# Two branch projections of a hybrid encoder, from 32-bit halves to scaled float16 halves

## The chip, the cores and the metric

One core of one Trainium2 chip runs the whole kernel. TensorE (PE) multiplies, with its weight loads shown as PEld; VectorE (DVE), ScalarE (ACT) and GpSimd (POOL) do the rest; SyncE (SP) issues nearly all DMAs, in the order of its own queue. The metric is the time of one execution on the device in microseconds, as the median of several runs.

## The reference, cut to what matters

One step of an encoder over 1024 prompt frames and 32 sample frames (1056 columns, `TT`), 1024 channels. Two branches are projected, mixed by sigmoid gates and projected once more:

```
def mixer_outputs(x, o_attn, conv, ga, gb, ma, mb, ln_g, ln_b, w_pa, w_pb, w_out):
    ya = (o_attn.reshape(B, T, ATTN_WIDTH) * jax.nn.silu(ga)) @ w_pa
    yb = (jax.nn.silu(layernorm(conv, ln_g, ln_b)) * jax.nn.silu(gb)) @ w_pb
    m = jax.nn.sigmoid(ma) * ya + jax.nn.sigmoid(mb) * yb
    return x + m @ w_out
```

All arrays are float32. `o_attn` comes from an attention with forget gates, `conv` from a causal depthwise convolution; `ga`, `gb`, `ma`, `mb` are columns of one input projection.

## The kernel before

Activations lie transposed: 128 channels by 1056 columns, eight such tiles `f` for 1024 channels. A product of 32-bit precision is made from halves: an operand is split into a high part `h` and a rest `l`, and `mms` issues for each of eight channel tiles `kt` the products wh·xh, wl·xh, wh·xl. An output tile is computed in three column pieces of 352 (`CH`), so 24 matmuls fill one PSUM bank piece and 72 one output tile.

Two kinds of halves are in use. The input projections (before about 1005 us) use float16 halves `xh`, `xl`: `Batch` squares and sums two weight tiles on ACT (`stage`), totals the sums over the partitions with a small PE matmul (`total`), takes a power of two from it on DVE (`power`), and makes scaled halves `wh` (`split`, on ACT, or on POOL where `sides["cast"]` says so) and `wl` (`rest`, three pieces on DVE); the result is scaled back by `inv` as the bank is read out. `begin` pops the next `Batch` from `plan` and spreads these steps over the beats of the product that runs (a beat, `beat`, is three matmuls). The last stages use 32-bit halves (F32R) that need no scaling: `split_w` copies a weight tile on ACT (L183) and subtracts on POOL in three pieces (L186).

The stages around the change:

- Until 980.5 us the attention runs, with 22 of 24 gate projections (`fills`) as filler between its matmuls. Its last matmuls are `po`; the gated results go to DRAM as `s_o` (L1336).
- From 980.5 us PE runs the last two fills, then `outproj("pa")`, then `outproj("pb")`, then the output projection (`Pair`, L1707). In this part only PE's order is written by hand; on the other engines and on SP a scheduler of the framework orders the instructions ahead of time.
- `a_half(f)` loads the attention's result from `s_o` into a buffer `a` (five such buffers, `bg`) and writes `ah` (ACT, L1515) and `al` (DVE, L1516).
- `ln_out(f)`, called in the course of `pa`, loads the convolution's `y` and the gate `g`, normalizes and multiplies in three DVE operations (L1524, L1525, L1528) and two Silu on ACT, and writes `c_h` on ACT (L1531) and `c_l` on POOL (L1532).
- `pa` multiplies its bank by (tanh(ma/2)+1) (`sma`, L1574) and stores it as `s_ya`; `pb` does the same with `mb` and adds `ya` (L1622, L1623), which gives twice the mixture. The factor 0.5 stands in the output stage (L1719, L1739).

Of the kernel before, what the change touches and what calls it, by code (L numbers as in the profile page):

```python
# [8 lines left out]
F32 = mybir.dt.float32  # L9
# [49 lines left out]
def build(tc, xT, xt, wv, wf, ckT, cv, clT, stT, vec, cst, yT, kT, vO, lfO, cpT, csT):  # L59
# [33 lines left out]
    class Batch:  # L93
# [34 lines left out]
        def total(self):  # L128
            pool, tag = totals[-1]
            held.add(id(self))  # L130
            self.ps = pool.tile([128, 512], F32, name="tot", tag=tag)
            if self.n == 2:
                nc.tensor.matmul(self.ps[:, :2], ones_b, self.topb, start=True, stop=True)
            else:
                for i in range(2):
                    nc.tensor.matmul(self.ps[:, 0:1], ones_b, self.topb[:, i:i + 1], start=(i == 0), stop=(i == 1))

        def power(self, ps=None, n=0):
            ps, n = (self.ps, self.n) if ps is None else (ps, n)
            held.discard(id(self))  # L140
            q, self.s, self.inv = [self.sc[:, 2 * i:2 * i + n] for i in range(3)]
            power(q, self.s, ps[:, :n], 77)
            nc.gpsimd.tensor_scalar(self.inv, q, back, 1.0, op0=ALU.mult, op1=ALU.mult)

# [139 lines left out]
    wx = pool("wx", 1, stack=pxp)  # L284
    xhome = [wx, wp, wp]
# [419 lines left out]
    makers += [lambda i=i: Batch(rest[i:i + 2]) for i in range(0, len(rest), 2)]  # L705
    rest = list(rest)
    plan.extend(m() for m in makers)
    firsts = {("ub", f) for f in range(1, 8)} | {("k", f) for f in range(8)} | set(rest[::2])
    totals.append((tr, "tr"))
    b1 = plan.pop(0)  # L710
# [785 lines left out]

    pjC = Banks3()
    bg = pool("bg", 5, stack=p3, side="right")
    rawp.extend(pool(f"rw{i}", 1, stack=p3, side="right") for i in range(2))
    psg2 = ExitStack()  # L1500
    sg2 = pool("sg2", 6, stack=psg2, side="right")
    whome[:] = [pool("w3", 1, stack=psg2, side="right"), wp, wp]

# [5 lines left out]
    nc.vector.tensor_mul(os_t, os_t, gs)  # L1509

    def a_half(f):
        a = big("a3")
        nc.sync.dma_start(a[:, :T], s_o[f, :, :T])
        nc.vector.tensor_copy(a[:, T:], os_t[:, f, :])
        nc.scalar.copy(ah[:, f, :], a)  # L1515
        nc.vector.tensor_sub(al[:, f, :], a, f32(ah[:, f, :]))  # L1516

    chl = []

    def ln_out(f):  # L1520
        y, g = big("y3"), big("g3")
        nc.sync.dma_start(y, s_y[f])
        nc.sync.dma_start(g, s_g["gb"][f])
        nc.vector.tensor_sub(y, y, mean)  # L1524
        nc.vector.tensor_mul(y, y, rstd)  # L1525
# [21 lines left out]
    def ln_step(f):  # L1547
        for g in LNO[f - 1]:
            ln_out(g)

    def outproj(g, rh, rl, mk, between=lambda f: None, order=range(8)):

        w = split_w(load_raw((g, order[0])))
        pss = [pjC.tile([128, CH], F32, name="pj", tag="pj") for _ in range(3)]
        for kt in range(KT):
            for c in range(3):
                mms(pss[c], w, rh, rl, csl(c), range(kt, kt + 1), kt == 0, kt == KT - 1)
        ev = mk(order[0])
# [8 lines left out]
    def mk_pa(f):  # L1567
# [4 lines left out]

        def ev(c, sl, ps):
            nc.vector.scalar_tensor_tensor(sma[c], sma[c], 1.0, ps, op0=ALU.add, op1=ALU.mult)  # L1574
# [39 lines left out]
    def mk_pb(f):  # L1614
        smb = mixed[f] = big("smb")
        nc.sync.dma_start(smb, s_g["mb"][f])
        nc.scalar.activation(smb, smb, AF.Tanh, scale=0.5)
        ya = big("ya")
        nc.sync.dma_start(ya, s_ya[f])

        def ev(c, sl, ps):
            nc.vector.scalar_tensor_tensor(smb[:, sl], smb[:, sl], 1.0, ps, op0=ALU.add, op1=ALU.mult)  # L1622
            nc.vector.tensor_add(smb[:, sl], smb[:, sl], ya[:, sl])  # L1623
            sm = slice(sl.start, min(sl.stop, HT if f < 4 else TT))
# [37 lines left out]
    class Pair:  # L1662
# [52 lines left out]
        def out(self, m, hf, x):  # L1715
            f = 2 * self.p + m

            def ev(sl, ps):
                nc.vector.scalar_tensor_tensor(x[:, sl], ps, 0.5, x[:, sl], op0=ALU.mult, op1=ALU.add)  # L1719
                nc.sync.dma_start(yT[f, :, hf * HT + sl.start:hf * HT + sl.stop], x[:, sl])  # L1720
# [6 lines left out]
        def first(self, w, x):  # L1727
            u = self.u
            yield from self.product(w, 0, quad(0, L), lambda sl, ps: nc.scalar.copy(u[:, sl], ps))
            later(3, lambda: nc.vector.scalar_tensor_tensor(x, u, 0.5, x, op0=ALU.mult, op1=ALU.add))  # L1730
            yield from self.product(w, 1, quad(4, L), self.out(0, 0, x))

        def second(self):
# [143 lines left out]
```

## Time and profile before

| | us |
|---|---|
| median of 3 runs | 1278.08 (1275.16 to 1278.91) |
| profiled execution, time on the device | 1275.56 |
| its span, first to last instruction | 1273.8 |
| PE busy | 1234.4 (97%) |
| DVE busy | 1009.4 (79%) |
| ACT busy | 745.7 (59%) |
| POOL busy | 628.5 (49%) |
| granted PE clock, mean | 0.993 |

A row of the groups has the line, engine, operation, output and input, the count, the busy time, the mean of one, and the idle time ahead. Matmuls overlap in the pipeline, so the time of one matmul (some 310 ns) is not its pitch: the pitch is read from starts that follow each other. The chain of waits names, from the end backwards, what the end waited for.

### The profile page before, as it was taken

The numbers are of one execution on the slowest core, as the hardware profiler recorded it, in microseconds if no ns is written. First come the engines' busy times: TensorE is split into PE (matmuls) and PEld (weight loads), VectorE is DVE, ScalarE is ACT, GpSimd is POOL, SyncE is SP. The second block draws the span as 40 slices with busy tenths as digits, with TensorE's granted clock in tenths as the row PEclk, the third lists the DMA queues.
The fourth block names the chain that finished last, engine by engine and source line by source line (L and its number), as shares of the span: only waits on it lengthen the run. The fifth ranks groups of instructions, "written<-read, shape, count | busy, mean of one in ns | idle before, by whom it ended". The sixth has DMA issues, their size and how long they took to land.

```text
span 1273.8 us, 24904 instructions
## 1 busy us (share of the span) xinstructions
PE 1234.4 (97%) x9276; PEld 924.3 (73%) x9276; DVE 1009.4 (79%) x1375; ACT 745.7 (59%) x1431; POOL 628.5 (49%) x579
## 2 busy tenths in 40 slices
PE   8999999999999999999999989989989999999998
PEld 5677786666666666666665655666656899999998
DVE  6799898888989989798998998876873694266764
ACT  6655655768677784456776666667764764233320
POOL 4058583728566561013554655534443285355662
PEclk9999999999999999999999999999999999999999
DMA  6345251423424247445989999989986987334462
GB/s 250 103 120 138 60 147 44 114 91 108 118 79 123 73 135 220 136 133 149 207 212 231 208 227 203 216 210 215 223 186 161 359 271 232 118 126 161 135 203 69
DMA packets 264410, 207.38 MB, mean 163 GB/s; under 512 B 186976, under 2 KB 228832, under 8 KB 264288
## 3 DMA queue, kind: packets, MB, share of 16 engines
q1 hardware_dynamic: 264144, 205.71, 59.7%
q8 instruction: 73, 1.20, 0.4%
q14 instruction: 49, 0.40, 0.1%
q10 hardware_dynamic: 144, 0.07, 0.0%
HBM read 110.84 MB, written 57.12 MB: 132 GB/s over the span
## 4 chain that ended last, share of the span: by engine, by line
PE 74%; DVE 9%; issue 5%; ACT 4%; DMA 3%; POOL 3%; SPq 0%; DVEq 0%; POOLq 0%; ACTq 0%
PE pj L194 53%; PE pjv L822 7%; PE pj L1707 6%; PE po L1319 2%; DVE wl L152 2%; DVE nm L1260 2%; DMA PT<-PH 2%; DVE PH L1290 2%; PE psS L1251 1%; POOL P L1287 1%; DVE y L386 1%; POOL PH L1288 1%; PE psS L1252 1%; ACT P L1266 1%; ACT PH L1281 1%
## 5 line engine op out<-in xcount | busy, mean ns | idle before, releaser
L194 PE MATMUL pj<-xl,wh 128*128 128x352 f16 (+2 forms) x1536 | 481.5, 313 | 1.3 <-DVE xl L608 1.3
L194 PE MATMUL pj<-xh,wh 128*128 128x352 f16 (+2 forms) x1536 | 481.9, 314 | 0.3 <-ACT xh L607 0.2
L194 PE MATMUL pj<-xh,wl 128*128 128x352 f16 (+2 forms) x1536 | 481.4, 313 | 0.1
L194 PEld LDWEIGHTS <-wh 128*128 128x128 f16 x3072 | 301.1, 98 | 163.1 <-issue 2.4
L386 DVE SCALAR_TENSOR_TENSOR y<-u,vec_t,y 128x1086 f32<-128x1086 f32 x240 | 358.2, 1493 | 4.0 <-ACT y L383 0.9
L194 PEld LDWEIGHTS <-wl 128*128 128x128 f16 x1536 | 150.5, 98 | 69.8 <-DVE wl L152 0.7
L1287 POOL TENSOR_SCALAR P<-P,nm 128x896 f32<-128x896 f32 (+3 forms) x64 | 66.7, 1042 | 188.0 <-ACT PH L1281 178.2
L152 DVE SCALAR_TENSOR_TENSOR wl<-raw,sc,wh 128x384 f16<-128x384 f32 x188 | 138.5, 758 | 23.5 <-ACT wh L149 22.2
L1266 ACT ACTIVATE P<-psS,nm 128x1024 f32<-128x1024 f32 (+7 forms) x128 | 94.5, 738 | 98.7 <-DVE nm L1260 36.7
L1260 DVE TENSOR_REDUCE nm<-psS 128x1 f32<-128x1024 f32 (+7 forms) x128 | 96.2, 751 | 44.8 <-PE psS L1253 28.3
L1281 ACT ACTIVATE PH<-P,nm 128x1024 f16<-128x1024 f32 (+7 forms) x128 | 98.5, 770 | 10.7 <-DMA PT<-PH 8.7
L186 POOL TENSOR_TENSOR wl<-raw,wh 128x384 fp32r<-128x384 f32 (+1 forms) x51 | 64.0, 1281 | 74.4 <-ACT wh L183 50.0
L1288 POOL TENSOR_TENSOR PH<-P,PH 128x896 f16<-128x896 f32 (+3 forms) x64 | 91.6, 1431 | 5.0
L953 POOL TENSOR_TENSOR sql<-sqf,sqh 128x352 fp32r<-128x352 f32 x48 | 53.2, 1108 | 68.0 <-ACT sqh L950 68.0
L1251 PE MATMUL psS<-KB,QB 128*128 128x512 f16 (+2 forms) x192 | 62.9, 328 | 18.6 <-ACT P L1266 18.4
L1290 DVE SCALAR_TENSOR_TENSOR PH<-P,nm,PH 128x896 f16<-128x896 f32 (+3 forms) x64 | 63.2, 988 | 15.0 <-ACT PH L1281 13.9
L822 PE MATMUL pjv<-vwh,xh 128*128 128x260 f16 x256 | 70.0, 274 | 0.0
L822 PE MATMUL pjv<-vwl,xh 128*128 128x260 f16 x256 | 70.0, 273 | 0.0
L822 PE MATMUL pjv<-vwh,xl 128*128 128x260 f16 x256 | 69.9, 273 | 0.0
L979 POOL TENSOR_TENSOR ql<-qn,qh 128x352 f16<-128x352 f32 (+1 forms) x48 | 62.7, 1321 | 9.4 <-ACT qh L978 9.2
L1319 PE MATMUL po<-PT,Vh 128*64 128x256 f16 (+1 forms) x640 | 58.2, 274 | 8.2 <-DMA PT<-PH 8.2
L120 ACT ACTIVATE junk<-raw 128x1024 bf16<-128x1024 f32 x62 | 65.1, 1049 | 0.1
(302 smaller groups left out, 2618.8 us busy)
## 6 DMA issues: line engine op xcount, KB each, us to landing
raw<-wf SPq DMA_DIRECT2D x92, 512.0 KB
kT<-kun SPq DMA_DIRECT2D x8, 528.0 KB
s_ga<-t SPq DMA_DIRECT2D x24, 176.0 KB
s_gb<-t SPq DMA_DIRECT2D x24, 176.0 KB
s_ma<-t SPq DMA_DIRECT2D x24, 176.0 KB
s_mb<-t SPq DMA_DIRECT2D x24, 176.0 KB
sma<-s_ma SPq DMA_DIRECT2D x24, 176.0 KB
y<-s_y SPq DMA_DIRECT2D x8, 528.0 KB
```

The lines of the kernel that those rows point to most:

```text
L152: nc.vector.scalar_tensor_tensor(wl[:, ks, :], raw[:, ks, :], self.s[:, i:i + 1], wh[:, ks, :], op0=ALU.mult, op1=ALU.subtract)
L194: nc.tensor.matmul(ps, a[:, kt, :], b(kt, sl), start=(first and n == 0), stop=(last and n == N - 1))
L386: t = nc.vector.scalar_tensor_tensor(y, u[:, i:i + CW], w, y, op0=ALU.mult, op1=ALU.add)
L822: nc.tensor.matmul(ps[:, :VC], a, b, start=(n == 0), stop=(n == 23))
L1260: nc.vector.tensor_reduce(self.nm[:, e:e + 1], self.ps[:, :self.w], axis=AX.X, op=ALU.max, negate=True)
L1266: nc.scalar.activation(self.P[:, :self.w], self.ps[:, :self.w], AF.Exp, bias=self.nm[:, e:e + 1], accum_out=self.nm[:, 2 + e:3 + e])
L1281: nc.scalar.mul(self.H[:, :n, 0, :], self.P3, self.f)
L1287: nc.gpsimd.tensor_scalar(self.P3, self.P3, f, 1.0, op0=ALU.mult, op1=ALU.mult)
L1288: nc.gpsimd.tensor_sub(self.H[:, :n, 1, :], self.P3, self.H[:, :n, 0, :])
L1290: nc.vector.scalar_tensor_tensor(self.H[:, :n, 1, :], self.P3, f, self.H[:, :n, 0, :], op0=ALU.mult, op1=ALU.subtract)
L1319: nc.tensor.matmul(po[64 * e:64 * e + 64, 128 * ii.start:256], v[:, j, 64 * e:64 * e + 64], pt[:, ii, e, j, x, :], start=(j == 0 and n == ...
L1707: nc.tensor.matmul(pss[c][:, :HC], a[:, k, :], x, start=(not more and kt == 0 and n == 0), stop=(kt == 3 and n == 2), skip_group_check=more)
```

## The change

Both branch projections get float16 halves of inputs and weights.

- The 16 weight tiles of `pa` and `pb` become eight more `Batch`es at the end of `plan`: squares on ACT, total on PE, `wh` on ACT, and `wl` now on DVE (L158 of the new kernel) where POOL made it before.
- The inputs get one scale for the whole operand (`Norm`): eight loads into eight `wide` buffers, eight squares on ACT with a sum, one PE matmul `ptot` over the sums (L1541), a reduction and two small steps on DVE, and only then eight high parts on ACT (L1548) and eight low parts on DVE (L1549). For `pa` this is emitted 18 beats before the end of the last fill; for `pb` in the second and third beat of output tile 6 of `pa`.
- `wide` is one set of eight buffers for both branches: a `y` of the convolution branch can be loaded only when the `a` of the same number has been split.
- `c_l` moves from POOL to DVE. The gate of `pb` is a Sigmoid instead of a Tanh, the scales back are multiplied in where `pb`'s banks are read (L1674, L1675), and the factor 0.5 leaves the output stage (three lines with a scalar become plain additions).

```diff
+        def square(self, f):
+            nc.scalar.activation(self.junk()[:, f, :].bitcast(BF16), self.x[f], AF.Square, accum_out=self.n8[:, f:f + 1])
+        def total(self):
+            ps = pjC.tile([128, CH], F32, name="ptot", tag="pj")
+            top, q, self.s = [self.sc[:, i:i + 1] for i in range(3)]
+            nc.tensor.matmul(ps[:, :8], ones_f, self.n8, start=True, stop=True)
+            nc.vector.tensor_reduce(top, ps[:, :8], axis=AX.X, op=ALU.add)
+            power(q, self.s, top, 77)
+            nc.gpsimd.tensor_scalar(self.back, q, 2.0 ** 100, 1.0, op0=ALU.mult, op1=ALU.mult)
+        def halves(self, h, l):
+            for f in range(8):
+                nc.scalar.mul(h[:, f, :], self.x[f], self.s)
+                nc.vector.scalar_tensor_tensor(l[:, f, :], self.x[f], self.s, h[:, f, :],
+                                               op0=ALU.mult, op1=ALU.subtract)
     def a_half(f):
-        a = big("a3")
+        a = norm_a.tile(f)
         nc.sync.dma_start(a[:, :T], s_o[f, :, :T])
         nc.vector.tensor_copy(a[:, T:], os_t[:, f, :])
-        nc.scalar.copy(ah[:, f, :], a)
-        nc.vector.tensor_sub(al[:, f, :], a, f32(ah[:, f, :]))
+        norm_a.square(f)
     def ln_out(f):
-        y, g = big("y3"), big("g3")
+        y, g = norm_c.tile(f), big("g3")
...
-        nc.scalar.copy(chl[0][:, f, :], y)
-        nc.gpsimd.tensor_sub(chl[1][:, f, :], y, f32(chl[0][:, f, :]))
+        norm_c.square(f)
     for f in range(8):
         a_half(f)
+    later(24 * len(fills) - 18, a_halves)
     while fills:
         last_gate()
...
+        if f == 6:
+            later(2, norm_c.total)
+            later(3, lambda: norm_c.halves(*chl))
     def outproj(g, rh, rl, mk, between=lambda f: None, order=range(8)):
-        w = split_w(load_raw((g, order[0])))
+        begin()
+        w = split.pop((g, order[0]))
...
-            nc.vector.scalar_tensor_tensor(smb[:, sl], smb[:, sl], 1.0, ps, op0=ALU.add, op1=ALU.mult)
-            nc.vector.tensor_add(smb[:, sl], smb[:, sl], ya[:, sl])
+            nc.vector.scalar_tensor_tensor(smb[:, sl], ps, inv, smb[:, sl], op0=ALU.mult, op1=ALU.mult)
+            nc.vector.scalar_tensor_tensor(smb[:, sl], ya[:, sl], sides["inv_a"][:, f:f + 1], smb[:, sl],
+                                           op0=ALU.mult, op1=ALU.add)
```

The scheduler makes new orders of SP, ACT and DVE from this. Two places matter.

SP at the end of the attention. Before, behind the last store `s_o<-ot` come two weight tiles, the sample gates `gs`, and the loads of `a` with other loads among them:

```order
L1336 DMA s_o<-ot 128x512
L175 DMA raw<-wf 128x1024 x2
L1508 DMA gs<-s_ga 128x8x32
L1513 DMA a_12871<-s_o 128x1024
L1044 DMA s_mb<-t 128x352
L1513 DMA a_12876<-s_o 128x1024
L1513 DMA a_12881<-s_o 128x1024
L1513 DMA a_12886<-s_o 128x1024
L1513 DMA a_12891<-s_o 128x1024
L175 DMA raw<-wf 128x1024
```

The same place on SP now, from the two weight tiles of the output projection (L181) on; `wide<-s_o` are the eight loads of `a`:

```order
L181 DMA raw<-wf 128x1024 x2
L1053 DMA s_mb<-t 128x352
L1345 DMA s_o<-ot 128x512
L1569 DMA g_13234<-s_gb 128x1056
L1569 DMA g_13355<-s_gb 128x1056
L1569 DMA g_13365<-s_gb 128x1056
L1569 DMA g_13475<-s_gb 128x1056
L1569 DMA g_13594<-s_gb 128x1056
L1053 DMA s_mb<-t 128x352
L1518 DMA gs<-s_ga 128x8x32
L1556 DMA wide<-s_o 128x1024 x6
L1053 DMA s_mb<-t 128x352
```

Five loads of `g`, which the convolution branch needs later, moved ahead of `gs` and of all loads of `a`; the last two loads of `a` follow the last row shown.

The low weight parts in the course of `pa`. Before, POOL made them, in turns with `c_l`:

```order
L1532 TENSOR_TENSOR c_l<-y_13183,c_h 128x1056
L186 TENSOR_TENSOR wl<-raw,wh 128x384 x2
L186 TENSOR_TENSOR wl<-raw,wh 128x256
L1532 TENSOR_TENSOR c_l<-y_13294,c_h 128x1056
L1532 TENSOR_TENSOR c_l<-y_13305,c_h 128x1056
L186 TENSOR_TENSOR wl<-raw,wh 128x384 x2
L186 TENSOR_TENSOR wl<-raw,wh 128x256
```

Now DVE makes them. Its rows for the second `Batch` of `pa` (output tiles 2 and 3), with the end of the convolution branch's work ahead of them (L1571 and L1574 are the products with `rstd` and `g`, L1626 reads `pa`'s banks, L175 is the scale of the weights):

```order
L1571 TENSOR_TENSOR wide<-wide,rstd 128x1056 x2
L1574 TENSOR_TENSOR wide<-wide,g_13475 128x1056
L1626 SCALAR_TENSOR_TENSOR sma<-sma,pj 128x352
L1574 TENSOR_TENSOR wide<-wide,g_13594 128x1056
L175 TENSOR_SCALAR sc<-sc 128x2
L1626 SCALAR_TENSOR_TENSOR sma<-sma,pj 128x352
L1574 TENSOR_TENSOR wide<-wide,g_13604 128x1056
L1574 TENSOR_TENSOR wide<-wide,g_13714 128x1056
L1574 TENSOR_TENSOR wide<-wide,g_13833 128x1056
L158 SCALAR_TENSOR_TENSOR wl<-raw,sc,wh 128x384 x2
L158 SCALAR_TENSOR_TENSOR wl<-raw,sc,wh 128x256
```

The low parts moved behind the whole convolution branch: between the scale of `a` and the first L158 row of this `Batch` DVE has the eight low parts of `a`, all 24 operations of L1570, L1571 and L1574, and the first six reads of `pa`'s banks. On PE, `ptot` stands behind 114 of the 168 matmuls of the fills that follow the last `po`; 54 more of the fills, 144 of output tiles 0 and 1, and one small total stand between it and the first matmul of output tile 2.

More of the change, by code (lines that the diff above doesn't have):

```diff
@@ L128, in total @@
         def total(self):
-            pool, tag = totals[-1]
+            pool, tag, width = totals[-1]
             held.add(id(self))
-            self.ps = pool.tile([128, 512], F32, name="tot", tag=tag)
+            self.ps = pool.tile([128, width], F32, name="tot", tag=tag)
             if self.n == 2:
@@ L142, in power @@
             power(q, self.s, ps[:, :n], 77)
-            nc.gpsimd.tensor_scalar(self.inv, q, back, 1.0, op0=ALU.mult, op1=ALU.mult)
+            g, f = self.keys[0][:2] if n == 2 else ("", 0)
+            if g == "pa":
+                self.inv = sides["inv_a"][:, f:f + 2]
+                later(8, lambda: nc.gpsimd.tensor_scalar(self.inv, q, sides["back_pa"], 0.5, op0=ALU.mult, op1=ALU.mult))
+            else:
+                nc.gpsimd.tensor_scalar(self.inv, q, sides["back_pb"] if g == "pb" else back, 1.0,
+                                        op0=ALU.mult, op1=ALU.mult)
         def high(self, i, wh, raw, ks):
@@ L277, in proj @@
             pass
+    pwx = ExitStack()
+    wx = pool("wx", 1, stack=pwx)
     pxp = ExitStack()
@@ L706, in build @@
     rest = list(rest)
+    last = [("pa", f) for f in range(8)] + [("pb", f) for f in PBO]
+    makers += [lambda i=i: Batch(last[i:i + 2]) for i in range(0, len(last), 2)]
     plan.extend(m() for m in makers)
-    firsts = {("ub", f) for f in range(1, 8)} | {("k", f) for f in range(8)} | set(rest[::2])
-    totals.append((tr, "tr"))
+    firsts = {("ub", f) for f in range(1, 8)} | {("k", f) for f in range(8)} | set(rest[::2]) | set(last[::2])
+    totals.append((tr, "tr", 512))
     b1 = plan.pop(0)
@@ L1497, in build @@
     pjC = Banks3()
+    totals.append((pjC, "pj", CH))
+    sides.pop("cast")
     bg = pool("bg", 5, stack=p3, side="right")
@@ L1500, in build @@
     psg2 = ExitStack()
+    pap = pool("pap", 1, stack=psg2, side="right")
+    ah = pap.tile([128, KT, TT], F16, name="ah")
+    al = pap.tile([128, KT, TT], F16, name="al")
     sg2 = pool("sg2", 6, stack=psg2, side="right")
-    whome[:] = [pool("w3", 1, stack=psg2, side="right"), wp, wp]
+    sides["inv_a"] = cp.tile([128, 8], F32, name="inv_a")
     def big(name):
@@ L1616, in mk_pb, with ev @@
         nc.sync.dma_start(smb, s_g["mb"][f])
-        nc.scalar.activation(smb, smb, AF.Tanh, scale=0.5)
+        nc.scalar.activation(smb, smb, AF.Sigmoid)
         ya = big("ya")
         nc.sync.dma_start(ya, s_ya[f])
-        def ev(c, sl, ps):
-            nc.vector.scalar_tensor_tensor(smb[:, sl], smb[:, sl], 1.0, ps, op0=ALU.add, op1=ALU.mult)
-            nc.vector.tensor_add(smb[:, sl], smb[:, sl], ya[:, sl])
+        def ev(c, sl, ps, inv):
+            nc.vector.scalar_tensor_tensor(smb[:, sl], ps, inv, smb[:, sl], op0=ALU.mult, op1=ALU.mult)
+            nc.vector.scalar_tensor_tensor(smb[:, sl], ya[:, sl], sides["inv_a"][:, f:f + 1], smb[:, sl],
+                                           op0=ALU.mult, op1=ALU.add)
             sm = slice(sl.start, min(sl.stop, HT if f < 4 else TT))
@@ L1729, in first @@
             yield from self.product(w, 0, quad(0, L), lambda sl, ps: nc.scalar.copy(u[:, sl], ps))
-            later(3, lambda: nc.vector.scalar_tensor_tensor(x, u, 0.5, x, op0=ALU.mult, op1=ALU.add))
+            later(3, lambda: nc.vector.tensor_add(x, x, u))
             yield from self.product(w, 1, quad(4, L), self.out(0, 0, x))
@@ L1738, in second @@
                 self.residual(m, hf, x)
-            half_of = lambda x, y: nc.vector.scalar_tensor_tensor(y, x, 0.5, y, op0=ALU.mult, op1=ALU.add)
+            plus = lambda x, y: nc.vector.tensor_add(y, y, x)
             sa, sb, z = [lambda i=i: self.w[i] for i in range(3)]
             yield from self.product(sa, 0, form(0), lambda sl, ps: nc.vector.tensor_add(u[:, sl], u[:, sl], ps))
-            later(4, lambda: half_of(u, x21))
-            later(5, lambda: half_of(u, x12))
+            later(4, lambda: plus(u, x21))
+            later(5, lambda: plus(u, x12))
             c = yield from self.product(sa, 1, form(1), lambda sl, ps: nc.vector.tensor_add(v[:, sl], u[:, sl], ps))
-            later(3, lambda: half_of(v, x22))
+            later(3, lambda: plus(v, x22))
             d = yield from self.product(sb, 0, quad(0, R), self.out(1, 1, x22))
```

37 lines of the change are left out of this document (25 added, 12 removed).

## Prediction

> **What bounds the kernel now.** I read the page's busy shares and its chain first, then the chain in order of time, then the stretches of the last 300 us.
>
> ```profile
> span 1273.8 us, 24904 instructions
> PE 1234.4 (97%) x9276; PEld 924.3 (73%) x9276; DVE 1009.4 (79%) x1375; ACT 745.7 (59%) x1431; POOL 628.5 (49%) x579
> PE 74%; DVE 9%; issue 5%; ACT 4%; DMA 3%; POOL 3%; SPq 0%; DVEq 0%; POOLq 0%; ACTq 0%
> 980.58 208.30 PE pj L194 x1320
> 1188.88 81.67 PE pj L1707 x672
> 1270.57 0.43 DVE r L1719
> ```
>
> From 980.58 us to the end the chain is PE alone: 1320 projection matmuls without a gap, then the 672 of the output projection. So a faster matmul here is worth its whole saving, and every wait of PE here is paid in full. The stretches (busy PE, PEld, DVE, ACT, POOL; clock, DMA share, GB/s) are the last fills, `pa` and `pb`:
>
> ```profile
> 980.60:1005.00 24.40, 24.40 (x165) 15.98 (x166) 10.48 (x16) 15.74 (x23) 5.45 (x6) 1.00 1.00 367
> 1005.20:1096.60 91.40, 91.40 (x577) 91.30 (x576) 58.51 (x49) 47.63 (x56) 54.03 (x29) 1.00 0.76 245
> 1096.70:1188.70 92.00, 92.00 (x580) 92.00 (x580) 49.50 (x69) 27.32 (x41) 46.49 (x43) 1.00 0.38 122
> ```
>
> PE is full in all three. DVE is at 58.51 of 91.40 us in `pa`, with POOL at 54.03. In the first stretch the DMA engines are full, at 367 GB/s: what is loaded there comes in the order in which SP asks for it.
>
> **The saving.** A matmul's pitch is read from starts and from evictions that follow each other. The first and the last of 45 float16 matmuls of 352 columns, and two evictions of `pb` that lie 48 of its 32-bit matmuls apart:
>
> ```profile
> 973.08 0.32 PE L194 MATMUL pj<-xh,wh 128*128 128x352 f16 x1
> 979.65 0.31 PE L194 MATMUL pj<-xl,wh 128*128 128x352 f16 x1
> 1135.50 0.52 DVE L1622 SCALAR_TENSOR_TENSOR smb<-smb,pj 128x352 f32<-128x352 f32 x1 [0.16 <-PE pj L194]
> 1143.13 0.52 DVE L1622 SCALAR_TENSOR_TENSOR smb<-smb,pj 128x352 f32<-128x352 f32 x1 [2.73 <-PE pj L194]
> ```
>
> Float16: 6.57 us over 44 steps, 149.3 ns. 32-bit: 7.63 us over 48, 159.0 ns. Two branches of 576 matmuls: 1152 x 9.7 ns = 11.2 us saved. This shape in float16 is in this trace, so the price is sure to some tenths of a us. The output projection stays 32-bit and saves nothing.
>
> **The first wait: the scale of `a`.** `ptot` stands behind 114 matmuls of the last fills: 980.5 + 114 x 0.1493 = 997.5 us. It needs the squares of all eight tiles of `a`, so the last load of `a` must have landed. Before, no PE instruction needed that so early:
>
> ```profile
> 981.13 0.32 SPq L1336 DMA_DIRECT2D s_o<-ot  x1
> 983.27 0.33 SPq L1513 DMA_DIRECT2D a<-s_o  x1
> 998.21 0.85 SPq L1513 DMA_DIRECT2D a<-s_o  x2
> 989.45 1.07 ACT L1515 CAST ah<-a 128x1056 fp32r<-128x1056 f32 x1 [0.88 <-DMA s_mb<-t]
> 1006.79 1.06 ACT L1515 CAST ah<-a 128x1056 fp32r<-128x1056 f32 x1
> a<-s_o SPq DMA_DIRECT2D x8, 512.0 KB
> raw<-wf SPq DMA_DIRECT2D x5, 512.0 KB
> g<-s_gb SPq DMA_DIRECT2D x3, 528.0 KB
> s_mb<-t SPq DMA_DIRECT2D x12, 176.0 KB
> s_o<-ot SPq DMA_DIRECT2D x2, 256.0 KB
> gs<-s_ga SPq DMA_DIRECT2D x1, 128.0 KB
> ```
>
> The first copy of `a` began at 989.45, the last at 1006.79. In the new order of SP there stand, up to and with the last load of `a`: two `raw` (1024 KB), three `s_mb` (528), `s_o` (256), five `g` (2640), `gs` (128) and eight `a` (4096): 8672 KB, 8.88 MB. At the 367 GB/s of the full stretch this takes 24.2 us, from 981.1 (when the last `s_o` can go, which ends the attention) to 1005.3; with one square (the 1.07 us of the same shape) the sum is there at 1006.4. The wait is 1006.4 - 997.5 = 8.9 us. The other bound: before, 2048 KB of `raw`, `gs`, the eight `a`, 1056 of `sma`, 528 of `s_mb` and `s_o` (8112 KB, 8.31 MB) took from 981.1 to 1006.8, which is 323 GB/s since loads from behind take a share; at that rate the sum comes at 1009.7, a wait of 12.2 us. I take 10, nearer the first, because the loads of `a` now follow each other closely; range 5.5 to 13. The Trainium skill (DMA: Bandwidth & Descriptors, Bandwidth) measured 425 GB/s for 16 MB. By that, an estimate, the wait would be 20.9 + 1.07 + 981.1 - 997.5 = 5.6 us and the whole 4.4 us less; the full stretch of this trace shows 367, and I keep that.
>
> **The second wait: the low weight parts of output tile 2.** From `ptot` to the first matmul of output tile 2 PE has 198 matmuls: 198 x 0.1493 = 29.6 us. DVE does its rows in order, and its first L158 row of that `Batch` stands behind the convolution branch. Prices:
>
> ```profile
> L1516 DVE TENSOR_TENSOR al<-a,ah x8: 1258/1259/1259, 990.6 to 1007.9; 128x1056 fp32r<-128x1056 f32 x8
> L1525 DVE TENSOR_TENSOR y<-y,rstd x8: 1244/1446/2069, 1011.2 to 1058.2; 128x1056 f32<-128x1056 f32 x8
> L1574 DVE SCALAR_TENSOR_TENSOR sma<-sma,pj x24: 506/511/524, 1016.5 to 1097.4; 128x352 f32<-128x352 f32 x24
> L152 DVE SCALAR_TENSOR_TENSOR wl<-raw,sc,wh x188: 464/612/2727, 10.9 to 976.1; 128x384 f16<-128x384 f32 x126, 128x256 f16<-128x256 f32 x62
> 998.05 0.88 ACT L1571 ACTIVATE sma<-sma 128x352 f32<-128x352 f32 x2
> 1029.77 1.25 DVE L1525 TENSOR_TENSOR y<-y,rstd 128x1056 f32<-128x1056 f32 x1
> 1030.93 0.51 DVE L1574 SCALAR_TENSOR_TENSOR sma<-sma,pj 128x352 f32<-128x352 f32 x1
> ```
>
> ACT has three Tanh of `sma` (0.49 each) and the first high part (1.07) ahead of DVE's first low part: 2.5 us. Then eight low parts of `a`: not in the trace in this form; at the 1.26 of L1516, 10.1 us. Then 24 operations at 1.25 us, the least of L1525, since POOL, with its 54.03 busy us beside that line's spread to 2.069, has almost nothing left here: 30.0. Six reads of banks at 0.51: 3.1. One low weight piece: 0.5. Sum 46.2, a wait of 16.6 us. Where operations follow each other freely the next starts some 0.08 us ahead of the printed end (1029.77 and 1030.93: 1.16 apart), which takes up to 2.5 us off: 14.1. With 1.446 for the 24 it would be 4.7 more: 21.3. I take 15.5: most rows wait for nothing, some for a row just ahead. This wait does not depend on the first, because both sides start at `ptot`.
>
> **The clock.** What a wait of over 3 us does to PE is in the trace:
>
> ```profile
> 936.70 0.31 PE L194 MATMUL pj<-xl,wh 128*128 128x352 f16 x1
> 940.54 0.58 PE L1251 MATMUL psS<-KB,QB 128*128 128x512 f16 x1 [3.53 <-ACT P L1266]
> 941.45 0.50 PE L194 MATMUL pj<-xh,wh 128*128 128x352 f16 x1
> 941.75 0.50 PE L194 MATMUL pj<-xh,wl 128*128 128x352 f16 x1
> 940.60:943.90 3.30, 3.30 (x20) 1.61 (x20) 1.75 (x3) 1.96 (x6) 0.00 (x0) 0.50 0.90 223
> 944.00:947.00 3.00, 3.00 (x22) 1.84 (x20) 1.99 (x4) 2.15 (x6) 1.36 (x2) 1.00 0.65 109
> ```
>
> After 3.53 us of idle time the granted clock is 0.50 until about 944 and 1.00 behind it; the same matmuls start 0.30 us apart instead of 0.149. 3.4 us at half speed are a loss of 1.7 us. After the first wait this loss lies beside DVE's work and only shortens the second wait; after the second it is paid. I add 1.7 (0 to 3.4). The Trainium skill (TensorE: Matmul & The Clock Gate, Part 1) has the gate look at free-running windows of about 3.4 us, so that a restart can fall inside one. By that, an estimate, up to two windows would run at half speed and the sum would be 1.7 us higher; the trace shows one.
>
> **What costs nothing, and its cover.** Squares and high parts of the weights on ACT (16 times two of about 1.05 us, less 16 copies it loses): ACT has 44 us free in `pa` and 65 in `pb`. Low weight parts later on, 2 x 1.9 us for each two output tiles of 21.5 us: DVE is free once the convolution branch is done. The scale of `c`: its squares end with the convolution branch, before output tile 3, and its eight high and low parts (8 x 1.26 = 10.1 us on DVE) have the 46 beats from the second of tile 6 to the end of `pa`, 46 x 0.448 = 20.6 us; if that cover went, PE would wait at the head of `pb` by what is over. Late reads of `pa`'s first banks: six of eight banks are held at the most, so PE finds one. Sigmoid for Tanh, a scalar form for an addition, additions for scaled ones in the output stage: the same shapes at 0.51 to 0.53 us, off the chain. Loads of `y` now wait until `a` is split; the first is asked for at the first low part's end and read four low parts (5 us) later.
>
> **Sum.** 10 + 15.5 + 1.7 - 11.2 = +16.0 us. Against the profiled execution, 1275.56, this gives 1291.6; the median of the runs shown is 1278.08, 2.5 higher. I say 1292.
>
> **The rivals.**
> Not slower: the second wait does not come, because DVE, with POOL quiet, does its 32 full-width operations faster than any row of before. It decides below (29.6 - 2.5 - 3.1 - 0.5) / 32 = 0.73 us each. Then 10 + 1.7 - 11.2 = +0.5: 1276, no change. Against it: the least of L1525 is 1.244 and that of L1516 1.258, with POOL idle beside some of them. 5 in 100.
> The first wait is small: the five `g` need nothing from the attention, and if their buffers come free early they are loaded while the DMA engines idle before 981. Without their 2.7 MB the sum is there 7.4 us earlier: 1284. Against it: SP asks in order, and they stand behind the last `s_o`. 15 in 100.
> The `y` come late: the first product of the convolution branch stands between the fifth and sixth low part of `a` on DVE; behind six `sma` and two `raw` (2.1 MB, 5.7 us at 367 GB/s) the first `y` may land 3 to 5 us after it is wanted, and everything behind it on DVE, with it the second wait, is longer by that: 1296. For it: the queue is full there. Against it: those eight are asked for during the first wait. 17 in 100.
> The matmuls don't gain: 32-bit ones carry their weight load, float16 ones have it as an instruction of its own. Then 1303. Against it are the 149.3 ns, with just such loads. 3 in 100.
>
> **How the numbers follow.** The forecast has 60 in 100. Its own ends are 5.5 + 14.1 - 11.2 = +8 and 13 + 21.3 + 3.4 - 11.2 = +26; the likely part and the two neighbouring rivals lie within 1284 and 1300, which I give as the range. 0.3% (some 4 us, about what a measurement of this kernel tells from no change) divides the rest: faster 3 in 100 (both waits far off at once), the same 5, slower 92.
>
> **What would show it.** Right: PE idle for about 10 us ahead of `ptot` near 997.5, its releaser ACT or a load of `a`; idle for about 15 us ahead of the first matmul of output tile 2, its releaser a low weight part on DVE, with DVE busy all the while; matmuls of both branches 149 ns apart; no wait at the head of `pb`. Wrong: DVE idle inside the second wait (the `y` are late), a `g` landed before 981 (the first wait shrinks), or a pitch near 159.

## Result, and the profile after

The changed kernel takes 1296.92 us (median of 4 runs, 1295.92 to 1299.53) against 1277.87 (4 runs) of the kernel before on the same chip: ratio 1.0156, 95% interval 1.0133 to 1.0178, 19.05 us slower. The forecast was 1292, the range 1284 to 1300.

The profiled execution took 1299.53 us, the slowest of the four. Part of that lies ahead of the change. These are the last matmuls of the attention, first in the kernel before, then after (start, duration, engine, line, operation, output and input):

```profile
980.35 0.22 PE L1319 MATMUL po<-PT,Vh 128*64 128x128 f16 x2
```

```profile
985.09 0.22 PE L1328 MATMUL po<-PT,Vh 128*64 128x128 f16 x2
```

Up to this row the two kernels do nearly the same work, and it came 4.74 us later in this one execution; in other runs of the changed kernel's variants it came at 979.0 to 983.9. So stages are compared from this row to the end of the span: 1273.8 - 980.35 = 293.4 us before, 1297.7 - 985.09 = 312.6 after. The difference, 19.2 us, agrees with that of the medians; this stretch is "the tail" below. PE's waits in the tail after the change (engine, line waited for, total, times, longest):

```profile
PE pj L200 <- ACT wh L155: 12.6, 1, 12.6
PE ptot L1541 <- ACT ah L1536: 11.7, 1, 11.7
PE pj L200 <- DVE wl L158: 0.2, 1, 0.2
```

Before there was none. The stretches of the tail after the change (columns as in the prediction):

```profile
985.50:1002.40 16.90, 16.90 (x115) 10.88 (x112) 0.74 (x2) 9.84 (x13) 0.00 (x0) 1.00 0.96 325
1002.40:1014.10 11.70, 0.05 (x2) 0.00 (x1) 4.03 (x17) 10.77 (x19) 0.00 (x0) 0.63 1.03 403
1014.70:1024.82 10.12, 10.12 (x55) 5.98 (x53) 8.71 (x10) 9.95 (x13) 0.46 (x2) 0.78 0.79 266
1044.50:1059.70 15.20, 2.46 (x15) 1.18 (x12) 13.38 (x18) 13.79 (x20) 2.38 (x1) 0.67 0.79 237
1059.70:1127.00 67.30, 67.24 (x442) 43.60 (x443) 28.57 (x54) 36.29 (x51) 1.56 (x7) 0.97 0.47 152
1127.00:1212.30 85.30, 85.30 (x577) 56.06 (x575) 56.47 (x98) 31.81 (x50) 22.93 (x28) 1.00 0.38 118
```

The second row is the first wait: PE idle, DMA full, ACT busy for 10.77 of 11.70 us. The fourth holds the second wait. Behind each the granted clock is under 1.00. The last row is `pb` without its first six matmuls. From the start of its first matmul to the start of its last, `pb` takes 85.9 us (1126.08 to 1211.97); before, it took 91.4 (1097.15 to 1188.56). The groups give its pitch: one of the three kinds of matmul, first and last start.

```profile
L200 PE MATMUL pj<-c_l,wh x192: 311/313/313, 1126.4 to 1212.0; 128*128 128x352 f16 x192
```

85.6 us over 573 steps are 149.4 ns. The saving is there in full; the waits cost more.

The first wait, row by row, on SP, ACT, DVE, ACT again and PE:

```profile
988.28 0.38 SPq L1345 DMA_DIRECT2D s_o<-ot  x1
994.19 1.28 ACT L1573 ACT_TABLE_LOAD   x1 [4.61 <-DMA g<-s_gb]
1000.70 1.08 ACT L1573 ACTIVATE g<-g 128x1056 f32<-128x1056 f32 x1 [0.32 <-DMA g<-s_gb]
1002.00 0.42 DVE L1519 TENSOR_TENSOR os_t<-os_t,gs 128x256 f32<-128x256 f32 x1 [16.16 <-DMA gs<-s_ga]
1003.34 1.08 ACT L1536 ACTIVATE ah<-wide 128x1056 bf16<-128x1056 f32 x1 [1.11 <-DVE sc L174]
1004.42 2.17 ACT L155 ACTIVATE wh<-raw,sc 128x1024 f16<-128x1024 f32 x2
1012.88 1.07 ACT L1536 ACTIVATE ah<-wide 128x1056 bf16<-128x1056 f32 x1
1014.10 0.60 PE L1541 MATMUL ptot<-n,ones_f 128*128 128x8 f32 x2 [11.65 <-ACT ah L1536]
```

The last `s_o` goes out at 988.28, 3.2 us after the attention's last matmul. On ACT a table load and the five Silu of the early `g` come first, from 994.19 to 1001.78. The sample gates `gs` land at 1002.0, the first square of `a` starts at 1003.34, and from there ACT runs without a gap: a square, two high weight parts, seven squares 1.06 us apart, none of which waits for a load. `ptot` comes when that row is through, 11.65 us after PE was ready.

The second wait: DVE's groups from 1016.6 to 1057.2 us, that whole stretch, and the rows around its end.

```profile
L1549 DVE SCALAR_TENSOR_TENSOR al<-wide,nsc,ah 128x1056 f16<-128x1056 f32 x8 | 10.1, 1311 | 1.3 <-ACT ah L1548 1.3
L1571 DVE TENSOR_TENSOR wide<-wide,rstd 128x1056 f32<-128x1056 f32 x8 | 9.9, 1250 | 0.0
L1570 DVE TENSOR_TENSOR wide<-wide,mean 128x1056 f32<-128x1056 f32 x8 | 9.8, 1251 | 0.0
L1574 DVE TENSOR_TENSOR wide<-wide,g 128x1056 f32<-128x1056 f32 x8 | 9.8, 1249 | 0.0
```

```profile
1016.60:1057.20 40.60, 29.89 (x193) 19.05 (x191) 40.60 (x40) 31.17 (x41) 3.32 (x2) 0.88 0.67 218
```

```profile
1053.69 3.59 DVE L1574 TENSOR_TENSOR wide<-wide,g 128x1056 f32<-128x1056 f32 x3
1057.92 2.17 ACT L155 ACTIVATE wh<-raw,sc 128x1024 f16<-128x1024 f32 x2
1059.09 3.00 DVE L158 SCALAR_TENSOR_TENSOR wl<-raw,sc,wh 128x384 f16<-128x384 f32 x6 [1.81 <-ACT wh L155]
1059.11 0.47 PE L200 MATMUL pj<-ah,wh 128*128 128x352 f16 x1 [12.62 <-ACT wh L155]
1059.76 0.47 PE L200 MATMUL pj<-ah,wl 128*128 128x352 f16 x1 [0.18 <-DVE wl L158]
```

DVE is busy for 40.60 of 40.60 us with the low parts of `a` and the convolution branch. Its row ends at 1057.3; ACT's high part begins at 1057.92, DVE's low part at 1059.09. PE is let go by the high part, so the page names ACT, but the two engines end within 2 us of each other. Which one holds the other, the page can't say.

### The profile page after: what moved, and what is told of

It reads as the page before. It is cut to its first block, busy times and chain, and to the rows that moved or that the text cites. A ratio compares the mean times of both kernels' runs of the same rounds, so it can differ in the third digit from the quotient of the medians.

```text
span 1297.7 us, 24983 instructions
## 1 busy us (share of the span) xinstructions
PE 1230.8 (95%) x9288; PEld 856.4 (66%) x9288; DVE 1021.6 (79%) x1453; ACT 781.3 (60%) x1495; POOL 558.0 (43%) x541
## 4 chain that ended last, share of the span: by engine, by line
PE 68%; DVE 10%; DMA 6%; issue 5%; ACT 5%; POOL 4%; SPq 1%; DVEq 0%; POOLq 0%; ACTq 0%
PE pj L200 48%; PE pjv L831 7%; PE pj L1761 6%; DMA PT<-PH 2%; PE po L1328 2%; POOL PH L1297 2%; DVE wl L158 2%; DVE nm L1269 1%; PE psS L1260 1%; DVE y L393 1%; PE psS L1261 1%; DVE PH L1299 1%; ACT PH L1290 1%; POOL P L1296 1%; ACT P L1275 1%
## 5 line engine op out<-in xcount | busy, mean ns | idle before, releaser
L200 PEld LDWEIGHTS <-wh 128*128 128x128 f16 x3840 | 377.5, 98 | 216.8 <-ACT wh L155 13.0
L200 PEld LDWEIGHTS <-wl 128*128 128x128 f16 x1920 | 188.5, 98 | 90.3 <-DVE wl L158 1.5
L158 DVE SCALAR_TENSOR_TENSOR wl<-raw,sc,wh 128x384 f16<-128x384 f32 (+1 forms) x236 | 167.7, 740 | 37.0 <-ACT wh L155 36.9
L1290 ACT ACTIVATE PH<-P,nm 128x1024 f16<-128x1024 f32 (+7 forms) x128 | 98.5, 770 | 12.1 <-DMA PT<-PH 10.2
L120 ACT ACTIVATE junk<-raw 128x1024 bf16<-128x1024 f32 x78 | 81.9, 1050 | 24.6 <-DMA raw<-wf 24.3
L962 POOL TENSOR_TENSOR sql<-sqf,sqh 128x352 fp32r<-128x352 f32 x48 | 56.6, 1182 | 64.8 <-ACT sqh L959 64.8
L200 PE MATMUL pj<-ah,wh 128*128 128x352 f16 x192 | 60.9, 317 | 12.6 <-ACT wh L155 12.6
L155 ACT ACTIVATE wh<-raw,sc 128x1024 f16<-128x1024 f32 (+1 forms) x58 | 64.2, 1123 | 14.3 <-DVE sc L175 14.3
L126 POOL CAST topb<-tops 128x2 bf16<-128x2 f32 x32 | 15.6, 488 | 131.3 <-ACT junk L120 131.1
```

Source lines behind the costliest of these rows:

```text
L120: nc.scalar.activation(junk[:, :raw.shape[1] * raw.shape[2]], raw.rearrange("p a b -> p (a b)"), AF.Square, accum_out=self.tops[:, i:i + 1])
L158: nc.vector.scalar_tensor_tensor(wl[:, ks, :], raw[:, ks, :], self.s[:, i:i + 1], wh[:, ks, :], op0=ALU.mult, op1=ALU.subtract)
L200: nc.tensor.matmul(ps, a[:, kt, :], b(kt, sl), start=(first and n == 0), stop=(last and n == N - 1))
L1290: nc.scalar.mul(self.H[:, :n, 0, :], self.P3, self.f)
```

## Experiments

The theory at this point: the change saves 11.2 us and pays for two rows that PE never waited for before, ACT's squares behind late loads (first wait) and DVE's convolution branch ahead of the weights' parts (second wait). Rivals: the late `gs` makes the first wait; ACT, not DVE, makes the second. The runs below were taken on several chips, so between rows the ratio and the tail compare better than the median.

| kernel | median us (range, runs) | ratio to before on the same chip (95%) | tail us |
|---|---|---|---|
| before | 1277.87 (1275.16 to 1278.91, 4) | | 293.4 |
| after | 1296.92 (1295.92 to 1299.53, 4) | 1.0156 (1.0133 to 1.0178) | 312.6 |
| `g` behind `a` | 1292.41 (1291.33 to 1294.27, 4) | 1.0119 (1.0100 to 1.0138) | 308.3 |
| weights first | 1284.00 (1282.17 to 1290.26, 5) | 1.0070 (1.0043 to 1.0096) | 299.4 |
| both | 1284.84 (1280.99 to 1285.28, 7) | 1.0045 (1.0030 to 1.0060) | 299.6 |
| `gs` early | 1296.49 (1293.80 to 1298.98, 4) | 1.0149 (1.0127 to 1.0171) | 313.0 |
| no squares of `c` | 1296.66 (1295.53 to 1298.88, 4) | 1.0145 (1.0128 to 1.0161) | 311.9 |
| DVE one less | 1290.30 (1289.27 to 1292.39, 4) | 1.0097 (1.0078 to 1.0116) | 306.2 |
| both, head of `pb` | 1276.58 (1273.10 to 1278.09, 12) | 0.9980 (0.9970 to 0.9990) | 291.6 |
| later total | 1273.85 (1271.22 to 1275.35, 6) | 0.9962 (0.9948 to 0.9977) | 289.6 |
| total 3 beats later | 1274.46 (1270.04 to 1278.06, 9) | 0.9973 (0.9955 to 0.9992) | 288.8 |
| total 5 beats later | 1275.20 (1272.26 to 1278.91, 12) | 0.9983 (0.9972 to 0.9994) | 291.3 |
| square first | 1270.58 (1268.51 to 1271.01, 5) | 0.9933 (0.9919 to 0.9946) | 285.9 |

**The five `g` behind the loads of `a`** (`tc.issue_after` puts an instruction behind a given one on that engine's queue):

```diff
-        nc.sync.dma_start(a[:, :T], s_o[f, :, :T])
+        sides["a_load"] = nc.sync.dma_start(a[:, :T], s_o[f, :, :T])
...
-        nc.sync.dma_start(g, s_g["gb"][f])
+        with tc.issue_after(sides["a_load"].ins):
+            nc.sync.dma_start(g, s_g["gb"][f])
```

> The five early loads of g are put behind the last load of a on SP; nothing else. Theory A (the scale of a waits for its loads, which queue behind g): 2640 KB less ahead of them, 7.4 us at 367 GB/s, so the wait ahead of ptot falls from 11.65 us to about 4 to 5 and the time by 6 to 8 us, to about 1290; the wait ahead of output tile 2 stays at 12 to 15 us, since DVE's work behind ptot is the same. Rival (PE reaches ptot at a time that something else sets, as the end of the attention or ACT's own queue): under 2 us.

PE's rows of this run:

```profile
1004.72 0.60 PE L1541 MATMUL ptot<-n,ones_f 128*128 128x8 f32 x2 [6.20 <-ACT ah L1536]
1048.89 0.48 PE L200 MATMUL pj<-ah,wh 128*128 128x352 f16 x1 [11.88 <-ACT wh L155]
```

The first wait falls from 11.65 to 6.20, the second stays (11.88), a small new one of 1.10 us comes at a weights' total `tot`, and the tail is 4.3 us shorter: less than the 6 to 8 expected. The five `g` are about half of the first wait. How they hold it, this run doesn't separate, because two things move: the loads on SP, and with them the Silu of `g` on ACT, which now begin behind the squares (table load at 1007.27). The first square starts 10.2 us after the attention's last matmul instead of 18.3, and it waits for a load of `a`.

**The weights ahead of the convolution branch**: ACT and DVE do the branch's rows behind the halves of `pa`'s weights 3 and, later, 5.

```diff
+            if self.keys[i:i + 1] in ([("pa", 3)], [("pa", 5)]):
+                sides["w_high"] = ins
...
     def ln_out(f):
+        with ExitStack() as behind_w:
+            for n in ("w_high", "w_low"):
+                if n in sides:
+                    behind_w.enter_context(tc.issue_after(sides[n].ins))
+            ln_work(f)
```

> Only the order on ACT and DVE: the convolution branch's work from its second tile on stands behind the halves of the weights of pa's output tiles 2 and 3, and from its fifth tile on behind those of tiles 4 and 5. Theory A (the second wait is a matter of the place in the queues): the wait ahead of output tile 2 goes, 12.6 us and some 1.7 us of half clock, and no new one comes, since the branch has until output tile 6; time about 1283. Rival (DVE or ACT simply have too much work in pa): the wait moves to a later output tile or to the head of pb and the time stays within 4 us of 1297.

```profile
1009.67 0.59 PE L1545 MATMUL ptot<-n,ones_f 128*128 128x8 f32 x2 [11.36 <-ACT ah L1540]
1108.26 0.32 PE L204 MATMUL pj<-c_h,wh 128*128 128x352 f16 x1 [1.57 <-ACT wh L155]
```

The second wait is gone and 13.2 us of the tail with it: the order on those two engines made it. A new wait of 1.57 us stands at the head of `pb`.

**Both edits.**

> Both edits. Theory A (two independent waits): both gains add up, 1297 - 7 - 14 = 1276, so about the time of before, with a rest of the first wait of 4 to 5 us against the saved 11.2 us: 1270 to 1277. Rival (the gains overlap): above 1280.

The sum of the two gains was not there: 1284.84. Against the run with the weights first, the wait at `ptot` is 4.9 us shorter (6.48), but the wait at the head of `pb` is 2.2 us longer, and behind it PE runs at half speed until 1114.01, a loss of some 2.8 us that the other run does not have. These two take back the gain. PE's and DVE's rows of this run at the head of `pb`:

```profile
1107.81 0.47 PE L204 MATMUL pj<-c_h,wh 128*128 128x352 f16 x1 [3.73 <-ACT wh L155]
```

```profile
1095.02 1.32 DVE L1553 SCALAR_TENSOR_TENSOR c_l<-wide,nsc,c_h 128x1056 f16<-128x1056 f32 x1 [10.99 <-ACT c_h L1552]
1102.04 3.77 DVE L1553 SCALAR_TENSOR_TENSOR c_l<-wide,nsc,c_h 128x1056 f16<-128x1056 f32 x3
1106.15 0.15 DVE L178 TENSOR_SCALAR sc<-tot 128x2 int32<-128x2 int32 x1
```

The scale `sc` of `pb`'s first weights, an operation of 0.15 us, stands on DVE behind eight low parts of `c`; without it ACT can't make the high part. The earlier PE arrives at `pb`, the more of this it waits for.

**`gs` early**: the load of `gs` and its product moved to the start of the attention.

> Only the load of the sample gates gs and its product move, to the start of the attention; the five g stay ahead of the loads of a. Theory A (the last load of a sets ptot): the wait ahead of ptot shrinks by 2 us at the most, time 1295 to 1297. Rival B (in the trace gs landed at 1002.0, the first square began at 1003.3 and ACT then worked without a pause, eight squares and two weight tiles, until 1014: the late gs and ACT's row set ptot): the squares follow the loads, the wait is 4 to 7 us shorter, time about 1291.

```profile
996.75 1.08 ACT L1535 ACTIVATE ah<-wide 128x1056 bf16<-128x1056 f32 x1 [0.25 <-DMA wide<-s_o]
1007.52 0.60 PE L1540 MATMUL ptot<-n,ones_f 128*128 128x8 f32 x2 [11.13 <-ACT ah L1535]
```

The first square now waits for a load of `a` itself, 0.25 us after ACT is through with the Silu of `g` and an eviction; ACT's row of 10.6 us follows as before, and the wait is 11.13. The rival falls: without the late `gs` the first square still comes 17.7 us after the attention's last matmul, against 18.3. The Silu of `g` and the first load of `a` are through within 0.3 us of each other here, so this run doesn't separate them either: both come of the five `g` ahead of `a`.

**No squares of `c`** (ACT has less to do, DVE the same; the scale of `c` is then a constant):

```diff
-        norm_c.square(f)
+        if f == 0:
+            nc.gpsimd.memset(norm_c.n8, 1000.0)
```

> The changed kernel without the eight squares of `c` on ACT (their sums are set to a constant, so the scale of `c` is fixed): 8 x 1.26 us less on ACT, five of them ahead of the weights' high part that released the second wait; nothing less on DVE. Theory (DVE's row sets the second wait, ACT's follows it): the high part comes up to 6 us earlier, but the low part stays behind DVE's row, which ended at 1057.3; the wait ahead of output tile 2 falls from 12.8 only to 11 to 12, and the time to 1294 to 1296. Rival (ACT's row sets it): the wait falls by 5 to 6 us, to about 7, and the time to 1289 to 1291.

```profile
1055.41 3.00 DVE L158 SCALAR_TENSOR_TENSOR wl<-raw,sc,wh 128x384 f16<-128x384 f32 x6
1055.43 0.48 PE L200 MATMUL pj<-ah,wh 128*128 128x352 f16 x1 [10.82 <-ACT wh L155]
```

ACT's high part (from 1054.24) and DVE's row end together here. The time, 1296.66, stays above the 1294 to 1296 expected: behind this wait PE runs at half speed for 5.5 us (1056.08 to 1061.57) against 3.8 in the changed kernel (1059.76 to 1063.51), so the tail is only 0.7 us shorter.

**One DVE operation less per tile** (the product with `rstd` is left out):

```diff
-        nc.vector.tensor_mul(y, y, rstd)
```

> The changed kernel without the multiplication of `y` by `rstd` (eight DVE operations of 1.17 us less; the convolution branch is then not scaled by it). ACT's work is the same, and its row has two squares more ahead of the weights' high part. Theory (DVE's row sets the second wait): it falls by 8 to 9.4 us, from 12.8 to 3.5 to 5, and the time to 1286 to 1289. Rival (ACT's row sets it): it falls by less than 3 us, and the time stays at 1293 or more.

```profile
1049.58 3.00 DVE L158 SCALAR_TENSOR_TENSOR wl<-raw,sc,wh 128x384 f16<-128x384 f32 x6 [4.54 <-ACT wh L155]
1049.60 0.48 PE L200 MATMUL pj<-ah,wh 128*128 128x352 f16 x1 [6.22 <-ACT wh L155]
```

With ACT eased, the wait falls by 1.8 us, and DVE starts its low part without an idle moment. With DVE eased it falls by 6.4 and stops there, because now DVE waits 4.54 us for ACT, with seven squares, and a table load and a Sigmoid of `pb`, ahead of the high part. The time, 1290.30, lies between theory and rival for the same reason. So DVE's row set the second wait and ACT's lay under 2 us behind it; further down ACT takes over at about 6 us. The page's releaser (ACT) was the last link of a chain that DVE held.

**Both edits, and the halves of `c` behind the halves of `pb`'s first weights** (`w_high` and `w_low` are then recorded for that tile too):

```diff
+    def c_halves():
+        with tc.issue_after(sides["w_high"].ins), tc.issue_after(sides["w_low"].ins):
+            norm_c.halves(*chl)
...
-            later(3, lambda: norm_c.halves(*chl))
+            later(36, c_halves)
```

> Both edits of the earlier runs (five `g` behind `a`; weights ahead of the convolution branch), and the halves of `c` are put behind the halves of pb's first weight tile, on ACT and on DVE. Theory: with both edits the second branch's head waited 3.73 us because the scale `sc` of its first weights stood on DVE behind eight low parts of `c` (`tot` was ready at 1093.8, `sc` began at 1106.15), and the slow clock after that wait cost 3.5 more (its span 89.1 us against 85.6). With `sc` ahead, the wait at the head of pb is under 0.5 us, pb takes 85.3 to 86, and the time falls from 1284.8 to 1278 to 1280. Rival: the gain of the two edits is not additive for another reason (a longer attention part in that run); then the wait goes and the time stays at 1283 to 1285. A second rival: the low parts of `c`, now 3 to 4 us later, are late themselves and PE waits inside the first tile of pb; then 1282 to 1285.

PE has one wait left in this tail, 6.31 us at `ptot`, and the time is 1276.58, somewhat below the 1278 to 1280 expected: the part that was missing from "both" stood at the head of `pb`.

**The total of `a` later, and ACT's table work behind the first half** (the Silu of `g` too; the step that scales `pa`'s weights back, which reads the scale, moves by as many beats and three more):

```diff
-    later(24 * len(fills) - 18, a_halves)
+    later(24 * len(fills) - 9, a_halves)
...
+            with tc.issue_after(sides["h_pa"].ins):
+                nc.scalar.activation(sma[c], sma[c], AF.Tanh, scale=0.5)
```

> As the run before, and the total of `a`'s squares on PE is asked for nine beats (4.0 us) later among the last fill matmuls, with ACT's tanh of `sma` and Silu of `g` (two table loads, 4.9 us between `ptot` and the first high part of `a`) put behind the first high part of `a`. Theory: the first wait is set by ACT's row of squares and then, a second time, by what stands between `ptot` and the first halves; the wait at `ptot` falls from 6.5 to about 2.5 us, the branch starts about 6 us earlier (some 27 us after the last attention matmul instead of 33), and the slow clock is not seen after `ptot`: 1271 to 1274, under the kernel before. Rival: the wait only moves from `ptot` to the first matmul of the branch, since the halves of `a` need as long as they did: 1277 to 1279.

```profile
1003.94 0.60 PE L1545 MATMUL ptot<-n,ones_f 128*128 128x8 f32 x2 [2.76 <-ACT ah L1540]
1004.00:1006.00 2.00, 2.00 (x8) 1.25 (x9) 0.47 (x3) 0.79 (x1) 0.46 (x2) 0.50 0.91 357
```

1273.85 lies in the theory's range, but not by its account. The clock fell after `ptot` all the same (second row, a stretch of this run: clock 0.50), and the first matmul of `pa` came 31.5 us after the attention's last, against 33.5 in the run before and not 27. These 2.0 us are what the tail gained. Which of the two edits gave them, one run with both doesn't say.

**The total three and five beats later still** (-6 and -4 in place of -9):

> As the kernel with the later total, whose wait of 2.76 us at `ptot` was followed by 5 us at a granted clock of 0.50, with the total three beats (1.34 us) later still. Theory: a wait of 2.76 us lowers the clock and one of 1.57 (the head of pb in the run with the weights ahead) did not; with some 1.4 us at `ptot` and under 1 us ahead of the first matmuls of the branch, the clock stays at 1.00, the branch starts about 3 us earlier (28.5 us after the last attention matmul instead of 31.5), and the time falls from 1273.9 to 1270 to 1272. Rival: the sum of the waits counts, not the longest; then the clock falls as before and the time stays at 1273 to 1275.

> The total five beats (2.2 us) later than in the kernel with the later total: the wait at `ptot` falls to some 0.5 us, and 1.5 to 2 us of waiting moves to the first matmuls of the branch, which need `ptot` + 3.8 us for the first halves. Theory as for the run beside it: 1270 to 1272, with the clock at 1.00. Rival: a wait between 1.57 and 2.76 us at that place lowers the clock, which then costs the slow matmuls of the branch itself: 1273 to 1275.

Both missed. With three beats the first matmul of `pa` comes 27.2 us after the attention's last instead of 31.5, earlier than expected, and the clock stays at 1.00; but the tail is only 0.8 us shorter. (Its 1274.46 is in the rival's range, without the slow clock that the rival needs.) PE's rows of that run, and of the run with five beats:

```profile
1008.14 0.39 PE L1545 MATMUL ptot<-n,ones_f 128*128 128x8 f32 x2 [1.50 <-ACT ah L1540]
1025.70 0.16 PE L133 MATMUL tot<-topb,ones_b 128*128 128x2 bf16 x1 [2.92 <-POOL topb L126]
```

```profile
1023.52 0.16 PE L133 MATMUL tot<-topb,ones_b 128*128 128x2 bf16 x1 [2.93 <-POOL topb L126]
```

The total of the next weights waits for a square (by way of a small cast on POOL) that now stands on ACT behind two table loads, six Tanh and a Silu, which I had moved there.

**That square ahead of the Tanh and Silu** (`sides["w_square"]`, the square of the next weight tile, in place of `sides["h_pa"]`; else as with three beats):

> As the run with the total three beats later, and ACT's tanh of `sma` and Silu of `g` stand behind the square of the next weight tile instead of behind the first high part of `a`. Theory: that run won the 4.3 us at the start of the branch (27.2 us from the last attention matmul to the branch, against 31.5) and gave 2.9 back at `tot` of the next weights, whose square stood on ACT behind two table loads and six tanhs; with the square ahead the wait at `tot` is gone, and the stretch from the last attention matmul to the end is 285 to 287 us instead of 288.8, the time 1270 to 1273. Rival: the tanhs, now later, hold back DVE's evacuation, the matmul banks fill up and PE waits for one; then the stretch stays at 288 to 289 and the time at 1273 to 1275.

```profile
PE ptot L1547 <- ACT ah L1542: 1.7, 1, 1.7
PE pj L206 <- DVE al L1555: 0.2, 1, 0.2
1007.20:1015.00 7.80, 7.60 (x51) 4.97 (x52) 6.06 (x8) 7.29 (x8) 0.46 (x2) 1.00 1.01 367
1015.00:1097.00 82.00, 82.00 (x555) 53.77 (x554) 60.36 (x88) 71.49 (x98) 5.84 (x9) 1.00 0.74 252
```

These are all waits of PE in the tail, and the stretches from `ptot` to the end of `pa`, with the clock at 1.00. 1270.58 us, as expected, ratio 0.9933 (0.9919 to 0.9946): 8.1 us faster than the kernel before, the tail 7.5 shorter. Of the 11.2 us of the float16 halves the waits that are left take 1.9, and the output stage, from the end of `pb` on, is 0.9 longer than before (86.0 against 85.1); the rest, about 0.9, is not traced.

## Why the prediction was right, and where it was off

By its own terms, from the tail after the change:

- **Saving**, -11.2: right. 149.4 ns between matmuls in `pb`.
- **First wait**, 10 taken, 12.25 measured (11.65 and the 0.60 of `ptot`): the mis-sized term. Its step "the last load, and one square" is wrong. The late loads end the wait for the first square, 18.3 us after the attention's last matmul (by way of `gs` in this run, by a load of `a` in the run with `gs` early); the wait for `ptot` ends with ACT's row of eight squares and two high weight parts, 10.6 us, which I had not added up because I took each square as done beside the next load. So the place was right, and the early `g` as its cause (`g` behind `a` takes 5.45 us off, with their Silu moved too), but much of the length was ACT's. That the size came close is in part luck: I gave to the loads nearly all the time that loads and squares shared. Two readings behind it were off as well. I counted from 0.8 us after the attention's last matmul, when the last `s_o` went out before; in the new order it went out after 3.2 us, behind a store of `s_mb` that went at 987.86, when ACT had evicted its bank. And the other bound's 323 GB/s took the start of the last copy of `a`, 1006.79, for a landing; that row waited for no load, because ACT was busy with a weight's copy until then, so 323 is only a lower bound of the rate.
- **Second wait**, 15.5 taken: from the end of `ptot`, 1014.70, to the second matmul of output tile 2, 1059.76, are 45.06 us; 199 matmuls at 0.1493 are 29.7, so PE lost 15.4. Of that 12.8 is idle time, and most of the rest the slow clock behind the first wait (54 matmuls in 10.12 us instead of 8.06), which shortened the idle time as the step said. The operations were 1.17 us apart, as the lower bound had it, and DVE was never idle in its row. That the sum came out at 15.4 is in part luck: DVE's row took 40.7 us and not 43.2, and the 1.8 us that DVE then waited for ACT's high part, which the sum did not have, came on top. The releaser was named wrongly (a low part on DVE; it was the high part on ACT), the cause rightly: the two runs that ease one engine show it.
- **Clock**, 1.7 taken: from 1059.76 to the last matmul of `pa`, 1125.93, are 66.17 us for 430 steps, 64.2 at full clock: 2.0 lost.
- **What costs nothing**: no wait at the head of `pb`, right, but its cover was partly the second wait itself. I looked at the halves of `c` and not at what they push back: with PE earlier, the weights' scale behind them on DVE became the wait.
- The output stage took 85.6 us instead of 85.1, which I had put at nothing.

12.25 + 15.4 + 2.0 - 11.2 + 0.5 = 18.95, against 19.2 measured. The forecast's 16.0 lacked 2.25 in the first wait and some tenths elsewhere. The other 2 of the 4.9 us between 1292 and 1296.92 come mostly from its base: I added to the profiled execution, 1275.56, and the median of the kernel before is 1277.87. Of the rivals, late `y` did not come (DVE has no idle time in its 40.60 us), no `g` landed before the attention's end, and the pitch fell as the trace before had it.

## What to carry to other kernels

A scale for a whole operand turns a pipeline into a barrier: the last load, the whole row of squares, the total and the first half stand one after the other, and what fills PE meanwhile must be sized to that sum, with each engine's row added up and not only the queue's end. Small operations (here a scale of 0.15 us on DVE, a square of 1.04 us on ACT) that stand in order behind long rows become waits as soon as PE gets earlier, so after each removed wait look for what is next in each engine's order. When a page names a releaser, ease its engine and its neighbour's in turn before calling either the cause.

## What the runs showed of the hardware

The attention's end moved between 979.0 and 985.1 us among the profiled executions of the changed kernel and its variants, which do the same up to there (one moved the small `gs` load); a comparison of one profiled execution each would have put 4.7 us of that on the change.

The clock does not go by the length of a wait alone. A wait of 2.76 us was followed at once by 0.50 (above), waits of 1.50 to 1.67 by nothing. The two waits of 2.92 and 2.93 us at the same `tot` differ; the stretches behind them, with three beats and with five, are these:

```profile
1025.70:1027.00 1.30, 1.30 (x10) 0.89 (x10) 1.10 (x2) 0.93 (x2) 0.85 (x1) 1.00 1.03 406
```

```profile
1023.50:1025.00 1.50, 1.48 (x11) 0.99 (x11) 0.33 (x2) 1.50 (x3) 0.27 (x1) 0.95 1.03 405
1025.00:1027.00 2.00, 2.00 (x9) 1.01 (x8) 0.00 (x0) 2.00 (x3) 0.00 (x0) 0.50 1.03 386
```

One run keeps 1.00, the other falls to 0.50 some 1.5 us after PE runs again. The Trainium skill (TensorE: Matmul & The Clock Gate, Part 1) has the clock set by free-running windows of about 3.4 us, so that it matters where in a window a wait falls; these rows agree with that, and my expectation of a fixed length of wait does not. The Trainium skill's table there has the clock fall after at least one idle window of that length; here waits of 2.76 and 2.93 us, shorter than one, were enough. After the two long waits of the changed kernel 2 us each were lost, at half speed for 4.6 us (1014.55 to 1019.15) and 3.8 (1059.76 to 1063.51). Over all the runs the half speed behind a wait lasted 2.6 to 5.8 us.
